# Order of VectorE and TensorE work in the first block of a two-block transformer kernel: convolution taps, pooling products, output product

## The chip, the cores and the metric

The kernel runs on one core of a Trainium2 chip. The metric is the device time of one execution in microseconds (us). The engines that matter here are TensorE (PE, matrix products, with a separate row PEld for loading weights), VectorE (DVE), ScalarE (ACT) and the queue of SyncE (SP), which issues the loads of weights. Each engine takes its instructions from a queue of its own; engines wait for each other by semaphores.

## The reference

The reference is a hybrid layer (the first block) followed by two more layers (the second block), on 512 tokens of width 1024, in float32. Only the mixing part of the first block is touched by the change:

```
h = rms_norm(x, norm1_g)
z = h @ w_in                       # split into 9 parts of 256 columns
y_pool  = pool_mixer(z_pool)       # moving means over 2, 4, 8, 16 tokens, then a 64x64 product per group
y_sconv = s_b * causal_dwconv(s_c * s_h, sconv_w)      # 3 taps
u       = causal_dwconv(c_a * sigmoid(c_g), conf_dw_w) + conf_dw_b    # 31 taps, each channel by itself
y_conf  = silu(layer_norm(u))
y_attn  = diff_attention(zq, zk, zv)                   # 4 heads, causal, two softmaxes per head
x = x + concat(y_pool, y_sconv, y_conf, y_attn) @ w_out
x = x + (silu(rms_norm(x) @ w_gate) * (rms_norm(x) @ w_up)) @ w_down
```

## The kernel before, in words

Activations are held with features on the 128 partitions and tokens along the free axis, so a stream of 256 features is two tiles `[:, 0]` and `[:, 1]` of 128x512. Every float32 product on TensorE is made of three passes: weight and activation are each split into a rounded part (`whi`, `hhi`) and a rest (`wlo`, `hlo`), and hi*hi, hi*lo and lo*hi are summed in PSUM. The split of weights is a ScalarE cast (L139) and a VectorE subtraction (L140, `wlo<-wraw,whi`); there are four buffers each of `whi` and `wlo`.

`layer1` works through the first block in this order: the gated stream of the 31-tap convolution (`u`), then the projections of values, keys and queries (L173, token-major), then the pooling stream `z`, the three streams of the short convolution, then the first output product `add_out(mixed[:4])`, which adds the pooling and short-convolution parts to `x`, and the second one, `add_out(mixed[4:])`, for attention (`yT`, mixed[4] and [5]) and convolution (`y`, mixed[6] and [7]). `mix` casts and splits such a part (L112 on ScalarE, L113 on VectorE) before it enters the output product. Each output product has 8 output tiles of 12 matmuls (4 parts x 3 passes), 96 matmuls in all, on three PSUM buffers `mm`; each tile ends in an addition to `x` on VectorE (L304).

Attention runs in the background: its stages are generators in `self.bg`, and `tick()`, called between groups of matmuls, lets the next stage emit its instructions. For keys and queries these are `heads_norm` (L484 to L486), `heads_stack` (`st`, L496 to L498) and `heads_turn` (transposes, L184 `psb<-keep,st`); after that, for each of 16 pairs of query block and head, `logits` (L536, then the VectorE pass L538 and the ScalarE exp L540), `turn` (transposes of `e`, copied to `pT`), `values` (`pso<-vtok,pT`, and for the last head of a block the normalisation of `ot`) and `finish` (transposes of `ot`, then `yT`, L590).

The 31-tap convolution `y` is one ScalarE instruction for the first tap and 30 VectorE instructions (L605) for the others, for each of the two tiles; 60 VectorE taps in all, each reading and writing the same `y`. When they are done comes a chain of its own, called the closing chain here: the sum over features on TensorE (L659, `psb<-y`), subtraction of the mean (L662), squares (L663), their sum (L667), the reciprocal root (L202 to L219), its spread over partitions (L223), and the scaling with SiLU (L674 to L678).

A scheduler decides at build time, from program order, priorities (`first()` and `chain()` raise them) and dependences, in which order each engine's queue stands; at run time each queue goes in that order. Tiles with a name in a pool are buffers in a ring: PSUM tiles `psb` have two buffers, handed out in program order, and the closing chain of `y`, the pooling product, and the transposes of attention all use them.

## Time and profile before

| what | us |
| --- | --- |
| median of 3 runs | 1217.9 (1216.07 to 1218.35) |
| time of the profiled execution | 1222.06 |
| its span, first to last instruction | 1220.3 |
| TensorE busy in the span | 1195.1 |
| VectorE busy in the span | 809.1 |
| ScalarE busy in the span | 622.0 |
| mean granted TensorE clock, share of full speed | 0.991 |

The profile gives for each engine its busy time, for each instruction its start and duration, and for an engine that sat idle what ended the wait. "Busy" on TensorE counts overlapping records, so TensorE is called busy where it is fed without a gap; what one matmul takes of TensorE's time is the distance from its start to the next one's.

### The profile page before, as it was taken

What the parts mean: (1) busy time and instruction counts of PE and PEld (TensorE: products, weight loads), DVE (VectorE), ACT (ScalarE), POOL (GpSimd) and SP (SyncE); (2) the same over time, 40 slices, a digit from 0 to 9 for tenths busy, and PEclk for the clock granted to TensorE, in tenths of its full rate; (3) what the DMA queues carried; (4) which work ended last, traced back from release to release, by engine and by line L of the source; (5) the groups of instructions that cost most, each with busy time, mean ns of one, the idle gap of its engine ahead of it and who ended that gap; (6) DMA issues with size and microseconds to landing.
All of it is one profiled execution on the core that took longest, in us unless ns stands there. A gap on an engine that the chain in (4) does not pass through costs nothing.

```text
span 1220.3 us, 18958 instructions
## 1 busy us (share of the span) xinstructions
PE 1195.1 (98%) x7234; PEld 1022.5 (84%) x7234; DVE 809.1 (66%) x1834; ACT 622.0 (51%) x1382; POOL 51.1 (4%) x77
## 2 busy tenths in 40 slices
PE   8989899999999999999999999999999999999996
PEld 6978788888888888888999899898899889876776
DVE  6899966444433444455799899666575576775775
ACT  6378656333323333344453345656563575575754
POOL 7000002000000000011000000000020000000000
PEclk9999999999999999999999999999999999999998
DMA  7422123223223332234221122222132213220122
GB/s 235 114 70 70 37 68 104 89 101 101 74 95 113 101 102 88 84 96 127 73 70 61 36 78 79 71 71 64 59 103 91 87 53 105 70 70 18 52 69 70
DMA packets 33308, 101.28 MB, mean 83 GB/s; under 512 B 4048, under 2 KB 6640, under 8 KB 33216
## 3 DMA queue, kind: packets, MB, share of 16 engines
q1 hardware_dynamic: 30528, 95.66, 24.6%
q0 software_dynamic: 880, 2.25, 0.7%
q10 hardware_dynamic: 1808, 2.16, 0.5%
q8 instruction: 57, 0.93, 0.3%
q14 instruction: 35, 0.29, 0.1%
HBM read 95.87 MB, written 3.10 MB: 81 GB/s over the span
## 4 chain that ended last, share of the span: by engine, by line
PE 86%; DVE 9%; ACT 3%; DMA 1%; issue 1%; SPq 0%; DVEq 0%; ACTq 0%
PE mm L154 68%; PE psb L184 3%; DVE wlo L140 2%; DVE y L605 2%; PE pso L1265 1%; DMA wraw<-in_w 1%; DVE sc L874 1%; PE pso L1018 1%; DVE m L873 1%; ACT whi L139 1%; PE psa L1146 1%; PE pso L1020 1%; PE pso L566 1%; PE mm L173 1%; DVE qk L749 1%
## 5 line engine op out<-in xcount | busy, mean ns | idle before, releaser
L154 PE MATMUL mm<-hhi,whi 128*128 128x512 f32 (+2 forms) x1280 | 432.8, 338 | 0.0
L154 PE MATMUL mm<-hlo,whi 128*128 128x512 f32 (+2 forms) x1280 | 427.5, 334 | 0.0
L154 PE MATMUL mm<-hhi,wlo 128*128 128x512 f32 (+2 forms) x1280 | 427.0, 334 | 0.0
L139 ACT CAST whi<-wraw 128x512 fp32r<-128x512 f32 x350 | 207.6, 595 | 328.4 <-PE mm L154 297.1
L140 DVE TENSOR_TENSOR wlo<-wraw,whi 128x512 fp32r<-128x512 f32 x350 | 233.9, 672 | 153.5 <-ACT whi L139 127.4
L154 PEld LDWEIGHTS mm<-hhi,whi 128*128 128x128 f32 x1280 | 242.4, 189 | 23.9 <-issue 2.2
L154 PEld LDWEIGHTS mm<-hlo,whi 128*128 128x128 f32 x1280 | 242.3, 189 | 21.8 <-issue 0.8
L154 PEld LDWEIGHTS mm<-hhi,wlo 128*128 128x128 f32 x1280 | 242.1, 189 | 21.8
L154 PE MATMUL mm<-mx,whi 128*128 128x512 f32 (+2 forms) x448 | 113.5, 342 | 3.5 <-ACT mx L112 3.3
L154 PEld LDWEIGHTS mm<-mx,whi 128*128 128x128 f32 x448 | 76.7, 192 | 15.7 <-ACT mx L112 4.1
L710 DVE TENSOR_TENSOR gu<-mm,rb 128x512 f32<-128x512 f32 x44 | 30.4, 691 | 68.8 <-PE mm L154 67.0
L154 PE MATMUL mm<-mx,wlo 128*128 128x512 f32 (+2 forms) x224 | 75.0, 335 | 0.0
L154 PE MATMUL mm<-hidh,wlo 128*128 128x512 f32 x176 | 68.5, 389 | 0.0
L154 PE MATMUL mm<-hidh,whi 128*128 128x512 f32 x176 | 68.5, 389 | 0.0
L154 PE MATMUL mm<-hidl,whi 128*128 128x512 f32 x176 | 68.5, 389 | 0.0
L247 POOL TENSOR_TENSOR acc<-acc,sq 128x528 f32<-128x528 f32 (+1 forms) x18 | 25.7, 1426 | 806.6 <-ACT sq L245 489.5
L316 DVE TENSOR_TENSOR tmp<-mm,rb 128x272 f32<-128x272 f32 (+2 forms) x76 | 35.6, 468 | 24.0 <-PE mm L154 22.8
L304 DVE TENSOR_TENSOR x<-x,mm 128x272 f32<-128x272 f32 (+2 forms) x72 | 36.7, 509 | 14.4 <-PE mm L154 13.2
L154 PEld LDWEIGHTS mm<-mx,wlo 128*128 128x128 f32 x224 | 42.8, 191 | 3.6
L605 DVE SCALAR_TENSOR_TENSOR y<-u,cols,y 128x512 f32<-128x512 f32 x60 | 42.5, 747 | 0.2
L154 PEld LDWEIGHTS mm<-hidh,wlo 128*128 128x128 f32 x176 | 33.0, 188 | 6.9
L154 PEld LDWEIGHTS mm<-hidh,whi 128*128 128x128 f32 x176 | 33.0, 188 | 6.9
(406 smaller groups left out, 1819.6 us busy)
## 6 DMA issues: line engine op xcount, KB each, us to landing
wraw<-in_w SPq DMA_DIRECT2D x145, 512.0 KB, 3.5
wraw<-in_w SPq DMA_DIRECT2D x16, 384.0 KB, 2.9
wraw<-in_w SPq DMA_DIRECT2D x16, 320.0 KB, 2.8
bh<-tab SPq DMA_DIRECT2D x16, 132.0 KB, 2.9
mx<-cqk SPq DMA_DIRECT2D x8, 132.0 KB, 2.4
x<-in_x SPq DMA_DIRECT2D x4, 256.0 KB, 7.3
x<-in_x ACTq DMA_DIRECT2D x4, 256.0 KB, 4.6
B<-tab POOLq DMA_DIRECT2D x4, 256.0 KB, 8.2
```

The lines of the kernel that those rows point to most:

```text
L139: self.nc.scalar.copy(hi[:, :w], raw[:, c])
L140: self.lo.tensor_tensor(out=lo[:, :w], in0=raw[:, c], in1=hi[:, :w].bitcast(F32), op=OP.subtract)
L154: nc.tensor.matmul(ps[b], lhsT=ww[i][:, f0:f0 + nf], rhs=aa[:, t0:t1], start=first and i == 0 and j == 0, stop=last and i == n - 1 and j == 2)
L173: nc.tensor.matmul(part(t), lhsT=aa[:, t0:t0 + nt], rhs=ww[i], start=u + i + j == 0 and t % 2 == 0, stop=u == 1 and i == 3 and j == 2, ski ...
L184: self.nc.tensor.transpose(out, in_, self.ident[:n, :n])
L247: e.tensor_tensor(out=acc[:, c0:c1], in0=acc[:, c0:c1], in1=sq[:, c0:c1], op=OP.add)
L304: nc.vector.tensor_tensor(out=x, in0=x, in1=p, op=OP.add)
L316: self.nc.vector.tensor_tensor(out=out[:, t0:t1], in0=p, in1=rb[:nf, t0:t1], op=OP.mult)
L566: nc.tensor.matmul(o[:, h * 64:h * 64 + 64], lhsT=pT[:, j * 128:(j + 1) * 128], rhs=vt[:, j, h * 64:h * 64 + 64], start=j == 0, stop=j == i)
L605: nc.vector.scalar_tensor_tensor(y[:, f], u[:, f, k:k + S], cw[:, f, k:k + 1], y[:, f], op0=OP.mult, op1=OP.add)
L710: nc.vector.tensor_tensor(out=t[:, g], in0=ps, in1=rbx, op=OP.mult)
L749: nc.vector.tensor_tensor(out=ll[a:a + 64], in0=src, in1=hh[r:r + 64].bitcast(F32), op=OP.subtract)
```

## The change

The arithmetic and the number of instructions of each kind stay as they are. What changes is the program order, and with it the order of the queues. (1) The taps of the convolution are emitted by `filler`, called from every `tick()`, at a pace given by a table (tick number, taps done); each is held, by a dependence that costs no semaphore, behind the VectorE instruction that stood last two ticks before. Taps that remain after the last projection are emitted together. (2) The sums and products of pooling are emitted before the short convolution's streams instead of after them. (3) `add_out` can begin with two output tiles at once, parts 0 and 1 of both first, then parts 2 and 3; both output products of the first block use it.

```
     def tick(self):
+        if self.filler:
+            self.filler()
         while self.bg:
...
+    def behind(self, ins, name):
+        if name and name != ins.ins.name:
+            self.tc.add_manual_dep(ins.ins, name, mybir.DependencyInfo(mybir.DependencyClass.NoSync, mybir.DependencyReason.DATA), reason="order")
...
+            if halves and u == 0:
+                (t0, t1), = toks
+                early = {f: [self.mm()[:, :t1 - t0]] for f in range(per)}
+                for h in range(2):
+                    for f in range(per):
+                        for i in range(h * nk // 2, (h + 1) * nk // 2):
+                            ah, al = mixed[i]
+                            for j, (ww, aa) in enumerate(((w[0], ah), (w[1], ah), (w[0], al))):
+                                nc.tensor.matmul(early[f][0], lhsT=ww[i][:, f * 128:f * 128 + 128], rhs=aa[:, t0:t1],
+                                                 start=i == 0 and j == 0, stop=i == nk - 1 and j == 2)
+                            self.tick()
...
+            taps = [(f, k) for f in range(2) for k in range(1, 31)]
+            paced = [(0, 0), (16, 14), (32, 28), (48, 35), (64, 40), (112, 60)]
+            done = []
+            def tap():
+                f, k = taps.pop(0)
+                return nc.vector.scalar_tensor_tensor(y[:, f], u[:, f, k:k + S], cw[:, f, k:k + 1], y[:, f], op0=OP.mult, op1=OP.add)
+            def filler():
+                done.append(self.last(mybir.EngineType.DVE))
+                t = len(done)
+                goal = np.interp(t, *zip(*paced))
+                while taps and 60 - len(taps) < goal:
+                    self.behind(tap(), done[-3] if t > 2 else None)
...
-            for f in range(2):
-                nc.scalar.activation(y[:, f], u[:, f, 0:S], AF.Identity, scale=cw[:, f, 0:1], bias=cb[:, f:f + 1])
-                for k in range(1, 31):
-                    nc.vector.scalar_tensor_tensor(y[:, f], u[:, f, k:k + S], cw[:, f, k:k + 1], y[:, f], op0=OP.mult, op1=OP.add)
...
             fproj(z[:, :, PADP:])
...
             fproj(None, evac=lambda f, ps: nc.scalar.copy(sc[:, f, PADS:], ps))
+            for f in range(2):
+                ps = self.ch("b")
+                nc.tensor.matmul(ps, lhsT=pw[:, f], rhs=z[:, f, PADP:], start=True, stop=True)
+                k = COLS["pscale"][0] + f
+                nc.scalar.mul(z[:, f, PADP:], ps, self.cols[:, k:k + 1])
+                mixed[f] = self.mix(z[:, f, PADP:], M, T)
             fproj(None, evac=lambda f, ps: nc.vector.tensor_tensor(out=sc[:, f, PADS:], in0=ps, in1=sc[:, f, PADS:], op=OP.mult))
             fproj(sb)
+            self.filler = None
+            while taps:
+                tap()
...
-            self.add_out(mixed[:4], X)
+            self.add_out(mixed[:4], X, halves=True)
...
-            self.add_out(mixed[4:], X, after)
+            self.add_out(mixed[4:], X, after, halves=True)
```

The queues of the changed kernel differ from those of before in the first block alone, and hold the same number of instructions of each kind there. Line numbers move: taps stand at L605 before and L509 now, weight splits at L140 and L152, matmuls at L154 and L166 (L319 where the two tiles are begun together), L484 to L497 become L535 to L548, L659 becomes L705, L667 becomes L713, L223 becomes L235, L184 becomes L196, L566 becomes L617, L304 becomes L332.

The first place is on VectorE, where the first stack of keys is prepared: `qss` is the sum of squares of a key half, `ktok` the normalised keys, `st` the stack that TensorE's transposes wait for. Before:

```order
L605 SCALAR_TENSOR_TENSOR y<-u,cols,y 128x512 [waits DVE_49] x5
L140 TENSOR_TENSOR wlo<-wraw,whi 128x512 [waits DMAHW5_49,PE_49,Activation_49]
L140 TENSOR_TENSOR wlo<-wraw,whi 128x512 [waits PE_49,Activation_49]
L605 SCALAR_TENSOR_TENSOR y<-u,cols,y 128x512 [waits DVE_49]
L605 SCALAR_TENSOR_TENSOR y<-u,cols,y 128x512
L605 SCALAR_TENSOR_TENSOR y<-u,cols,y 128x512 [waits DVE_49] x3
L484 TENSOR_REDUCE qss<-qsq 128x16 [waits Activation_49]
```

The same place on VectorE in the changed kernel, up to the same reduction:

```order
L509 SCALAR_TENSOR_TENSOR y<-u,cols,y 128x512 [waits DVE_49] x6
L152 TENSOR_TENSOR wlo<-wraw,whi 128x512 [waits DMAHW5_49,PE_49,Activation_49]
L152 TENSOR_TENSOR wlo<-wraw,whi 128x512 [waits PE_49,Activation_49]
L509 SCALAR_TENSOR_TENSOR y<-u,cols,y 128x512 [waits DVE_49] x4
L535 TENSOR_REDUCE qss<-qsq 128x16 [waits Activation_49]
```

Counted from the start, 28 taps stood ahead of this reduction and 25 do now; the number of weight splits ahead of it is the same.

The second place is on VectorE, between the last logits of attention (`e,st<-psa`, shown as ISA) and the first weights of the first output product. Before, from the last logits pass on (`sb` is the short convolution's last stream, and `mx<-sb,mx`, `mx<-z,mx` are second halves of `mix`):

```order
L538 ISA e,st<-psa,B_272 128x512 [waits PE_49]
L538 ISA st 128x1
L547 SCALAR_TENSOR_TENSOR e<-e,rd 128x512 [waits DVE_49]
L219 SCALAR_TENSOR_TENSOR os<-rt,ry 128x4 [waits DVE_49]
L646 TENSOR_TENSOR sb<-sb,mx 128x512
L578 TENSOR_TENSOR ot<-ot,os 128x256 [waits DVE_49]
L545 RECIPROCAL rd<-st 128x2 [waits Activation_49]
L645 SCALAR_TENSOR_TENSOR mx<-mx,cols 128x512
L113 TENSOR_TENSOR mx<-sb,mx 128x512 [waits Activation_49]
L546 TENSOR_SCALAR rd<-rd,st,rowp 128x1 [waits DVE_49]
L440 TENSOR_TENSOR sb<-mm,rb 128x512 [waits PE_49]
L547 SCALAR_TENSOR_TENSOR e<-e,rd 128x512 [waits DVE_49]
```

In the changed kernel, from the last logits pass to the first weight split:

```order
L589 ISA e,st<-psa,B_272 128x512 [waits PE_49]
L589 ISA st 128x1
L598 SCALAR_TENSOR_TENSOR e<-e,rd 128x512 [waits DVE_49]
L629 TENSOR_TENSOR ot<-ot,os 128x256 [waits DVE_49]
L698 TENSOR_TENSOR sb<-sb,mx 128x512
L596 RECIPROCAL rd<-st 128x2 [waits Activation_49]
L468 TENSOR_TENSOR sb<-mm,rb 128x512 [waits PE_49]
L125 TENSOR_TENSOR mx<-sb,mx 128x512 [waits Activation_49]
L597 TENSOR_SCALAR rd<-rd,st,rowp 128x1 [waits DVE_49]
L698 TENSOR_TENSOR sb<-sb,mx 128x512 [waits DVE_49]
L598 SCALAR_TENSOR_TENSOR e<-e,rd 128x512 [waits DVE_49]
L152 TENSOR_TENSOR wlo<-wraw,whi 128x512 [waits DMAHW7_49]
```

One step of the short convolution (L645) is out of this stretch; the weight split still stands behind both products of `sb` and the last `e`. After it four taps were left in the kernel before; in the changed one 13 are left, two at a time between the additions to `x` of the first output product.

The third place is on TensorE, in the first output product (`mm<-mx`), where the sum over features of `y` (`psb<-y`) and the sum of its squares (`psb<-ones,ysq`) stand. Before, this was after 21 of the 96 matmuls, and matmuls stood between the steps:

```order
L659 MATMUL psb<-y,m_107 128x512 [waits DVE_49]
L154 MATMUL mm<-mx,whi 128x512 x2
L154 MATMUL mm<-mx,wlo 128x512
L154 MATMUL mm<-mx,whi 128x512 x2
L154 MATMUL mm<-mx,wlo 128x512
L154 MATMUL mm<-mx,whi 128x512 x2
L667 MATMUL psb<-ones,ysq 128x1 [waits Activation_49]
L154 MATMUL mm<-mx,wlo 128x512
L154 MATMUL mm<-mx,whi 128x512
L667 MATMUL psb<-ones,ysq 128x1 [waits Activation_49]
```

In the changed kernel the same steps stand after 92 of the 96 matmuls:

```order
L705 MATMUL psb<-y,m_107 128x512 [waits DVE_49]
L166 MATMUL mm<-mx,wlo 128x512
L166 MATMUL mm<-mx,whi 128x512 x2
L166 MATMUL mm<-mx,wlo 128x512
L713 MATMUL psb<-ones,ysq 128x1 [waits PE_49,Activation_49]
L713 MATMUL psb<-ones,ysq 128x1 [waits Activation_49]
L713 MATMUL psb<-ones,ysq 128x1 x6
L235 MATMUL psb<-keep,yr 128x128 [waits DVE_49]
L235 MATMUL psb<-keep,yr 128x128 x3
```

Behind these rows TensorE's queue goes on with the last two transposes of `e`, the last two products with the values, the last transposes of `ot`, and only then the second output product, whose first matmul waits for the cast of `yT`:

```order
L196 MATMUL psb<-keep,e 128x128 [waits DVE_49]
L196 MATMUL psb<-keep,e 128x128 x3
L617 MATMUL pso<-vtok,pT 128x64 [waits Activation_49]
L617 MATMUL pso<-vtok,pT 128x64 x3
L617 MATMUL pso<-vtok,pT 128x64 [waits Activation_49]
L617 MATMUL pso<-vtok,pT 128x64 x3
L196 MATMUL psb<-keep,ot 128x128 [waits DVE_49,PE_49]
L196 MATMUL psb<-keep,ot 128x128
L319 MATMUL mm<-mx,whi 128x512 [waits Activation_49]
```

Before, 52 of the 96 matmuls of the first output product stood behind the last product with the values; now none does.

## Rows read from the trace of the kernel before

**Rows 1.** Page, busy time of TensorE and its weight loads in the span:

```profile
PE 1195.1 (98%) x7234; PEld 1022.5 (84%) x7234; DVE 809.1 (66%) x1834; ACT 622.0 (51%) x1382; POOL 51.1 (4%) x77
```

**Rows 2.** Waits of TensorE, whole span: us in total, times, longest:

```profile
PE mm L154 <- ACT mx L112: 3.3, 1, 3.3
PE psb L184 <- ACT st L498: 3.1, 1, 3.1
```

**Rows 3.** Busy by stretch: PE, PEld, DVE, ACT, POOL, granted clock, DMA share, GB/s:

```profile
64.00:68.00 4.00, 0.90 (x9) 0.84 (x9) 4.00 (x11) 3.19 (x10) 0.00 (x0) 1.00 0.32 124
68.00:72.00 4.00, 4.00 (x24) 4.00 (x23) 4.00 (x7) 1.95 (x5) 0.00 (x0) 0.57 0.43 131
148.00:152.00 4.00, 3.82 (x8) 2.62 (x9) 3.96 (x8) 0.63 (x2) 0.00 (x0) 0.50 0.39 131
152.00:156.00 4.00, 4.00 (x15) 3.17 (x15) 2.98 (x5) 0.62 (x1) 0.00 (x0) 0.80 0.42 131
155.81:175.28 19.47, 19.47 (x107) 15.80 (x106) 11.99 (x24) 12.51 (x28) 0.00 (x0) 1.00 0.16 52
205.00:1205.00 1000.00, 995.01 (x6126) 853.35 (x6127) 628.42 (x1428) 484.00 (x1060) 18.45 (x17) 1.00 0.25 79
```

**Rows 4.** VectorE in order of time before the first stack: start, us, instruction:

```profile
51.11 4.73 DVE L605 SCALAR_TENSOR_TENSOR y<-u,cols,y 128x512 f32<-128x512 f32 x7
56.95 3.40 DVE L605 SCALAR_TENSOR_TENSOR y<-u,cols,y 128x512 f32<-128x512 f32 x5
60.27 0.68 DVE L484 TENSOR_REDUCE qss<-qsq 128x16 f32<-128x512 f32 x1
66.25 0.42 DVE L497 TENSOR_TENSOR st<-ktok,st 128x256 fp32r<-128x256 f32 x1
```

**Rows 5.** TensorE at the first stack, in order of time:

```profile
67.17 1.09 PE L184 MATMUL psb<-keep,st 128*128 128x128 f32 x8 [3.10 <-ACT st L498]
```

**Rows 6.** VectorE after the last logits, in order of time:

```profile
140.54 0.68 DVE L538 CUSTOM_DVE_ANT_0 e<-psa,B 128x512 f32<-128x512 f32 x1
143.21 0.73 DVE L645 SCALAR_TENSOR_TENSOR mx<-mx,cols 128x512 f32<-128x512 f32 x1
146.86 1.29 DVE L140 TENSOR_TENSOR wlo<-wraw,whi 128x512 fp32r<-128x512 f32 x2
```

**Rows 7.** TensorE from the last logits to the first output product, in order of time:

```profile
139.15 0.71 PE L536 MATMUL psa<-kT,qT 128*128 128x512 f32 x2
141.09 1.88 PE L650 MATMUL psb<-z,pw 128*128 128x512 f32 x4
148.17 2.03 PE L154 MATMUL mm<-mx,whi 128*128 128x512 f32 x3 [3.32 <-ACT mx L112]
```

**Rows 8.** Chain that ended last, merged: start, TensorE's time, what:

```profile
155.97 0.86 PE psb L659 x2
159.49 1.46 PE psb L667 x14
162.45 0.61 PE psb L223 x4
163.98 0.52 PE psb L184 x4
165.42 0.87 PE pso L566 x8
208.33 131.72 PE mm L154 x581
```

**Rows 9.** The closing chain and attention's last block, in order of time:

```profile
155.81 1.02 PE L659 MATMUL psb<-y,m 128*128 128x512 f32 x2
167.67 0.42 DVE L574 TENSOR_TENSOR ot<-pso,rd 128x256 f32<-128x256 f32 x1 [3.29 <-PE pso L566]
169.63 0.63 ACT L195 ACTIVATE ysq<-ysq 128x512 f32<-128x512 f32 x1
174.81 0.47 ACT L590 ACTIVATE yT<-psb,cols 128x256 f32<-128x256 f32 x1 [0.29 <-PE psb L184]
```

More of the change, by code (lines that the diff above doesn't have):

```diff
@@ L100, in finish, with last @@
             self.tick()
+    def last(self, engine):
+        return next((i.name for i in reversed(self.nc.cur_bb.bb.instructions) if i.engine == engine), None)
+    def behind(self, ins, name):
+        if name and name != ins.ins.name:
+            self.tc.add_manual_dep(ins.ins, name, mybir.DependencyInfo(mybir.DependencyClass.NoSync, mybir.DependencyReason.DATA), reason="order")
     def row(self, name):
@@ L288, in mix, with add_out @@
         return hi, lo
-    def add_out(self, mixed, toks, after=None, ws=None):
+    def add_out(self, mixed, toks, after=None, ws=None, halves=False):
         nc = self.nc
@@ L296, in add_out @@
             w = ws[u] if ws else self.weights(nk, per * 128)
-            for f in range(per):
-                ps = [self.mm()[:, :t1 - t0] for t0, t1 in toks]
-                self.f_acc(ps, w, f * 128, 128, mixed, toks)
+            early = {}
+            if halves and u == 0:
[9 more added lines that the diff above has]
+                            self.tick()
+            for f in range(per):
+                if early:
+                    ps = early[f]
+                else:
+                    ps = [self.mm()[:, :t1 - t0] for t0, t1 in toks]
+                    self.f_acc(ps, w, f * 128, 128, mixed, toks)
                 kt = u * per + f
@@ L611, in layer1 @@
             fproj(z[:, :, PADP:])
-            rb2 = p.tile([128, S], F32, name="rb2")
-            nc.scalar.square(rb2, rbx)
-            PADS = 2
-            sb, sc, sh = G(S, "sb", "qtok"), X2(PADS + S), X2(S)
-            nc.gpsimd.memset(sc[:, :, :PADS], 0.0)
-            fproj(None, evac=lambda f, ps: nc.scalar.copy(sc[:, f, PADS:], ps))
-            fproj(None, evac=lambda f, ps: nc.vector.tensor_tensor(out=sc[:, f, PADS:], in0=ps, in1=sc[:, f, PADS:], op=OP.mult))
-            fproj(sb)
             mixed = [None] * 8
@@ L639, in layer1 @@
                     nc.vector.tensor_tensor(out=z[:, f, PADP:], in0=a[:, PADP:], in1=z[:, f, PADP:], op=OP.subtract)
+            rb2 = p.tile([128, S], F32, name="rb2")
+            nc.scalar.square(rb2, rbx)
+            PADS = 2
+            sb, sc, sh = G(S, "sb", "qtok"), X2(PADS + S), X2(S)
+            nc.gpsimd.memset(sc[:, :, :PADS], 0.0)
+            fproj(None, evac=lambda f, ps: nc.scalar.copy(sc[:, f, PADS:], ps))
+            for f in range(2):
+                ps = self.ch("b")
[3 more added lines that the diff above has]
+                mixed[f] = self.mix(z[:, f, PADP:], M, T)
+            fproj(None, evac=lambda f, ps: nc.vector.tensor_tensor(out=sc[:, f, PADS:], in0=ps, in1=sc[:, f, PADS:], op=OP.mult))
+            fproj(sb)
+            self.filler = None
+            while taps:
+                tap()
+            with self.chain():
                 nc.vector.tensor_tensor(out=sc[:, :, PADS:], in0=sc[:, :, PADS:], in1=rb2[:, None, :].to_broadcast([128, 2, S]), op=OP.mult)
@@ L647, in layer1 @@
                     mixed[2 + f] = self.mix(sb[:, f], M, T)
-            for f in range(2):
-                ps = self.ch("b")
-                nc.tensor.matmul(ps, lhsT=pw[:, f], rhs=z[:, f, PADP:], start=True, stop=True)
-                k = COLS["pscale"][0] + f
-                nc.scalar.mul(z[:, f, PADP:], ps, self.cols[:, k:k + 1])
-                mixed[f] = self.mix(z[:, f, PADP:], M, T)
             ones = self.m1
```

8 lines of the change are left out of this document (5 added, 3 removed).

## The prediction

> **What bounds the kernel now.** I read the page first: TensorE is busy 1195.1 of 1220.3 us [rows 1]. After the first block it is fed without a gap, 995.01 of 1000 us between 205 and 1205 [rows 3], so time lost or won in the first block is neither made up nor lost again later; the end moves by just that much. The waits of TensorE come next. Two are above 3 us, both in the first block: 3.1 for the first stack of keys and 3.3 for the first part of the output product [rows 2]. The windows then show what follows each: the granted clock is at 0.57 in 68 to 72 and at 0.50 and 0.80 in 148 to 156 [rows 3], that is TensorE at the lower of its two levels (1.2 instead of 2.4 GHz) for a while after it starts again. That costs 4 x 0.43 = 1.7 us after the first wait and 4 x 0.50 + 4 x 0.20 = 2.8 after the second. The two waits with their aftermath are 1.7 + 3.1 = 4.8 and 2.8 + 3.3 = 6.1 us, 10.9 in all, which is the most that a better order can win here. Third, I read where the closing chain of the convolution runs: from the sum over features at 155.81 [rows 9] to the last piece of attention, yT, at 174.81 + 0.47 = 175.28. In this stretch TensorE is busy 19.47 of 19.47 us [rows 3]: the chain is long, but matmuls of the first output product stand between its steps.
>
> **The change, part by part.** No instruction is added or dropped, so each term is a wait that shrinks or appears.
>
> *Taps paced, first wait.* VectorE works without a pause before the first stack: five taps from 56.95 to the reduction at 60.27 are 0.66 us each [rows 4]. In the new order 3 of 28 taps stand behind that reduction, so it starts 2.0 earlier. From it to the start of the transposes were 67.17 - 60.27 = 6.9 us [rows 4, 5]. In this stretch ScalarE's queue now has small operations of the second half of the keys ahead of the first copy of the stack; I take 0.5 of the 2.0 as lost to them, so that the transposes start 1.5 earlier. Three matmuls of the query projection moved from ahead of the transposes to behind them; half of 131.72 / 581 = 0.227 us [rows 8] each, 0.34 together, so the wait begins that much earlier. The wait shrinks by 1.5 - 0.34 = 1.1, to 2.0 us. Bounds: 0.6 (another 0.5 lost) and 1.7. Whether the lower clock still follows a wait of 2.0 us no row shows; the bounds are 0 and 1.7 won, and I take 0.8. Term: -1.1 - 0.8.
>
> *Pooling first, two tiles at once: second wait.* Before, the wait ended when the casts of the pooling parts came, which stood last; now parts 0 and 1 are there early. But the first matmul with wlo needs the split of the weights on VectorE, and in the new order that split still stands behind the whole tail of the last logits. Before, the last logits pass started at 140.54 and the split at 146.86, 6.3 later [rows 6]. One step of the short convolution, 0.73, and about 0.5 of small waits around it go out of the stretch: 5.1. Counted from TensorE's last logits at 139.15 [rows 7], the split starts at 1.4 + 5.1 = 6.5 and is done 0.65 later (half of 1.29), at 7.2. TensorE had 5.7 us of work of its own from there (to 148.17 - 3.32 = 144.85). Of this the pooling products (1.88 by their row [rows 7], of which I take 1.7, since the end overlaps with what follows) and half of the sum of y, 0.9 as the other half [rows 8], are now done earlier at the same price, and four matmuls with parts 0 and 1 come in, 0.9: 4.0 us. It waits 7.2 - 4.0 = 3.2 instead of 3.3 [rows 7]. The cover was brought forward together with the work that it would cover. Term: -0.2, with a little for a short second wait; bounds 0 and -6.1, if the wait closes with its aftermath.
>
> *Taps held back: the closing chain.* 13 taps are left for the first output product instead of 4, and VectorE's queue puts them between the additions to x, so the sum over features stands behind 92 of the 96 matmuls. TensorE's queue then holds the steps of the chain one after another, then the last transposes and products of attention, which share the two buffers psb with them, then the second output product. I add up the path from the start of the sum over features:
> - to the end of the spread of the reciprocal root: 162.45 + 0.61 - 155.81 = 7.25 [rows 8, 9], and 0.15 since a cast of weights that waits for the end of the product now stands ahead of the squares on ScalarE: 7.4;
> - to the end of the last product with the values: 167.67 - 163.06 = 4.6 before; 4.4 without casts of weights in between;
> - to yT: 175.28 - 167.67 = 7.6 before [rows 9]. One addition to x and three weight splits on VectorE (about 0.6 each) stand elsewhere now: 5.2;
> - the cast of yT, as long as another 128x512 pass on ScalarE: 0.63 [rows 9].
>
> That is 17.6 us. TensorE's own work in it: 0.86 for the sum, four matmuls 0.9, 16 sums of squares at 1.46 / 14 = 1.7, the spread 0.61, 12 transposes at 0.52 / 4 = 1.6, 16 products at 0.87 / 8 = 1.7 [rows 8], together 7.4. It stands idle for 17.6 - 7.4 = 10.2 us. Bounds: 7.5 if four passes of y's SiLU between attention's steps (some 0.65 each) delay nothing, and 12.7 if the path is as long as before (175.28 - 155.81 + 0.63 = 20.1). A row for the clock after broken work like this is missing; the nearest are the 1.7 and 2.8 us after the two waits, and I take 2.2, with 0 and 2.8 as bounds. Term: +10.2 + 2.2.
>
> That VectorE comes to the last tap in time I check by a sum: 13 taps at 0.66, seven additions and eight splits at about 0.6 make 17.6 us against 92 matmuls at 0.227 = 20.9, so TensorE's pace sets the start of the chain and no more is lost there.
>
> Behind a matmul that waits, nothing runs on TensorE: in the 3.10 us ahead of the transposes [rows 5] the query projection's matmuls stood ready behind them. The Trainium skill (PSUM - Partial Sum Buffer, Engine vs sequencer instructions) states the same as a rule, matmuls start and complete in program order. It speaks against this change: by it the products of attention that stand behind the closing chain cannot fill its waits. If they could pass, the sum would be lower by about the 4.4 us of the second step; I keep the sum by the rows.
>
> **Sum.** -1.1 - 0.8 - 0.2 + 10.2 + 2.2 = +10.3 us. The profiled execution took 1222.06 us for a span of 1220.3, 4.2 above the median; the terms are differences, so I put the sum on the median: 1217.9 + 10.3 = 1228.2. With all bounds one way (the closing of the second wait is a rival, below) the forecast's own range is -1.7 - 1.7 - 0.2 + 7.5 = +3.9 to -0.6 + 12.7 + 2.8 = +14.9, 1222 to 1233.
>
> **The rivals.**
> - *The second wait closes.* If the split of the first weights comes before TensorE needs it (it decides below 4.0 us after the last logits' start, where I have 7.2), 6.1 are won instead of 0.2: 1222.3. For it: pooling's parts are ready early. Against: the order of VectorE's queue. Chance 0.12.
> - *The closing chain stays hidden, and the change wins.* If TensorE finds the steps ready as it did before, with no wait in 19.47 us [rows 3], the 12.4 us fall away, the first wait's -1.9 to -2.8 stays: 1215 to 1216, faster. It decides where the path from the sum to yT's cast is below 9.5 us. Against: 17.6 by the rows, and only four matmuls stand between. Chance 0.05.
> - *The waits only change places.* Path at its low bound and no lower clock (+7.5), second wait closed (-6.1), first wait as forecast (-1.9): 1217.4, no change. Chance 0.05.
> - *VectorE is late.* If the 13 taps end after TensorE's 92 matmuls (17.6 us become more than 21), the chain starts later, by some 3 us: 1231. For it: VectorE is busy through all of 64 to 72 [rows 3] and has little slack in this block. Against: the sum above. Chance 0.08.
>
> **How the numbers follow.** The forecast has 0.70. A difference under 0.2%, 2.4 us, can't be told from no change. Faster by more than that: half of the second rival and the low end of the first, 0.04. Within: the rest of the second and the third: 0.08. Slower: all else, 0.88. The range, 1221.5 to 1232.5, takes in the first rival's centre and most of the fourth, and leaves out the other two.
>
> **What would show it.** Right: among TensorE's waits one or more around the end of the first output product, together about 10 us, for ScalarE and VectorE steps of y and ot; the longest before the last transposes of ot and before the first matmul of the second product; a lower granted clock right behind it; the first wait at about 2 us; the wait at the start of the first output product still about 3 us, now for wlo on VectorE. The prediction fails if TensorE passes the closing chain with under 6 us of waits, or if the wait for the first weights is gone.

## The result, and the profile after

The changed kernel took 1235.05 us (median of 4 runs, 1231.56 to 1240.64) against 1218.12 for the kernel before (4 runs): a ratio of 1.0139, interval 1.0114 to 1.0164. It is slower by 17 us. The two profiled executions lie closer together: span 1232.1 against 1220.3 us, 11.8 more.

The waits of TensorE in the changed kernel, first those that answer to [rows 2] and then those around the end of the first output product (us in total, times, longest):

```profile
PE psb L196 <- DVE ot L629: 4.3, 1, 4.3
...
PE psb L196 <- ACT st L549: 2.2, 1, 2.2
PE mm L319 <- DVE wlo L152: 2.0, 1, 2.0
...
PE psb L235 <- DVE yr L231: 1.5, 1, 1.5
...
PE mm L319 <- ACT mx L124: 1.2, 1, 1.2
...
PE psb L713 <- ACT ysq L709: 1.0, 1, 1.0
PE mm L166 <- DVE sb L468: 0.9, 1, 0.9
PE psb L196 <- ACT yT L641: 0.6, 1, 0.6
PE psb L196 <- ACT e L591: 0.4, 1, 0.4
```

The first wait (`st`) shrank from 3.1 to 2.2. The second one, 3.3 for a cast of `mx` before, is now 0.9 for `sb` and 2.0 for the split `wlo`. The other six are new. The one of 0.4 for `e` ends at 101.05, in an earlier part of attention; the five around the end of the first output product are 4.3 + 1.5 + 1.2 + 1.0 + 0.6 = 8.5 us (added unrounded). TensorE in order of time shows where they stand, from the end of the first output product to the start of the second:

```profile
172.02 1.02 PE L705 MATMUL psb<-y,m 128*128 128x512 f32 x2
...
174.97 2.24 PE L713 MATMUL psb<-ones,ysq 128*128 128x1 f32 x16 [1.00 <-ACT ysq L709]
178.68 1.07 PE L235 MATMUL psb<-keep,yr 128*128 128x128 f32 x4 [1.46 <-DVE yr L231]
...
180.73 1.77 PE L196 MATMUL psb<-keep,e 128*128 128x128 f32 x8 [0.56 <-ACT yT L641]
182.52 2.11 PE L617 MATMUL pso<-vtok,pT 128*128 128x64 f32 x16
188.94 0.66 PE L196 MATMUL psb<-keep,ot 128*128 128x128 f32 x2 [4.31 <-DVE ot L629]
190.82 0.79 PE L319 MATMUL mm<-mx,whi 128*128 128x512 f32 x1 [1.21 <-ACT mx L124]
```

The second piece of the sum over features stood at 155.81 with matmuls of the product around each step of the chain [rows 9]; now it stands at 172.02, and the product ends before the chain does. The windows (columns as in [rows 3]; the third number from the right is the granted clock) show what that does to the clock:

```profile
64.00:68.00 4.00, 1.91 (x9) 1.91 (x10) 3.98 (x10) 3.08 (x10) 0.00 (x0) 0.76 0.05 22
68.00:72.00 4.00, 4.00 (x31) 4.00 (x30) 3.27 (x6) 2.21 (x6) 0.00 (x0) 0.81 0.43 131
148.00:152.00 4.00, 2.61 (x6) 2.13 (x7) 4.00 (x8) 0.62 (x1) 0.00 (x0) 0.50 0.14 19
152.00:156.00 4.00, 4.00 (x13) 3.11 (x13) 1.27 (x3) 0.62 (x1) 0.00 (x0) 0.64 0.72 243
176.00:180.00 4.00, 2.54 (x17) 2.22 (x17) 0.55 (x3) 0.88 (x4) 0.00 (x0) 0.84 0.41 131
180.00:184.00 4.00, 3.42 (x21) 2.97 (x21) 1.06 (x2) 3.29 (x7) 0.00 (x0) 0.73 0.00 0
184.00:188.00 4.00, 0.63 (x6) 0.49 (x5) 2.16 (x5) 3.85 (x11) 0.00 (x0) 0.70 0.00 0
188.00:192.00 4.00, 1.84 (x5) 1.25 (x6) 1.93 (x6) 2.33 (x5) 0.00 (x0) 0.50 0.00 0
192.00:196.00 4.00, 4.00 (x12) 3.08 (x11) 1.29 (x3) 0.33 (x1) 0.00 (x0) 0.52 0.02 4
```

From 176 to 196 the granted clock is between 0.84 and 0.50, that is at its lower level for most of that time, with a return to full speed around 184. Such windows also give an account of the whole span. In steps of 4 us I add up TensorE's idle time (length less busy) and the time lost to the lower clock (busy x (1 - clock); in 192 to 196, 4.00 x 0.48 = 1.9). What is left of the span should be the same work at full clock in every trace of the same kernel. In the two kernels that were traced twice, and in two others, it agrees to 0.4 us:

| trace | span | idle 56-224 | lower clock 56-224 | lower clock elsewhere | idle elsewhere | left |
| --- | --- | --- | --- | --- | --- | --- |
| before | 1220.3 | 6.6 | 4.6 | 2.1 | 18.6 | 1188.4 |
| before, second trace | 1220.3 | 8.2 | 4.5 | 0.1 | 19.0 | 1188.5 |
| changed | 1232.1 | 14.6 | 8.3 | 1.7 | 19.2 | 1188.3 |
| changed, second trace | 1231.2 | 12.5 | 7.1 | 3.6 | 19.4 | 1188.6 |
| taps done by tick 64 | 1223.3 | 10.0 | 3.9 | 1.7 | 19.5 | 1188.2 |
| attention first, late pace | 1222.5 | 4.5 | 3.2 | 7.2 | 19.1 | 1188.5 |

In the other seven kernels without added matmuls what is left lies between 1186.8 and 1190.6, so from kernel to kernel this account closes within some 2 us, not within tenths.

The 11.8 us between the first two traces are 8.0 of idle time in the first block, 3.7 of lower clock there, and small change elsewhere (0.6 idle, -0.4 lower clock).

### The profile page after: what moved, and what is told of

Same layout as the page of the kernel before. It is cut to its first block, busy times and chain, and to the rows that moved or that the text cites. A ratio compares the mean times of both kernels' runs of the same rounds, so it can differ in the third digit from the quotient of the medians.

```text
span 1232.1 us, 18962 instructions
## 1 busy us (share of the span) xinstructions
PE 1198.2 (97%) x7234; PEld 1024.7 (83%) x7234; DVE 812.9 (66%) x1834; ACT 622.7 (51%) x1382; POOL 51.2 (4%) x77
## 4 chain that ended last, share of the span: by engine, by line
PE 85%; DVE 9%; ACT 4%; DMA 1%; issue 1%; SPq 0%; DVEq 0%; ACTq 0%
PE mm L166 66%; PE psb L196 4%; DVE wlo L152 2%; DVE y L509 1%; PE pso L1311 1%; PE mm L319 1%; DMA wraw<-in_w 1%; DVE sc L920 1%; PE pso L1064 1%; DVE m L919 1%; PE psa L166 1%; ACT whi L151 1%; PE psa L1192 1%; PE pso L1066 1%; DVE qk L795 1%
## 5 line engine op out<-in xcount | busy, mean ns | idle before, releaser
L166 PE MATMUL mm<-hhi,whi 128*128 128x512 f32 (+2 forms) x1280 | 432.6, 338 | 0.0
L166 PE MATMUL mm<-hlo,whi 128*128 128x512 f32 (+2 forms) x1280 | 426.9, 334 | 0.0
L166 PE MATMUL mm<-hhi,wlo 128*128 128x512 f32 (+2 forms) x1280 | 426.2, 333 | 0.0
L152 DVE TENSOR_TENSOR wlo<-wraw,whi 128x512 fp32r<-128x512 f32 x350 | 234.1, 673 | 155.1 <-ACT whi L151 128.9
L166 PEld LDWEIGHTS mm<-hhi,whi 128*128 128x128 f32 x1280 | 241.7, 189 | 24.1 <-issue 2.4
L166 PEld LDWEIGHTS mm<-hlo,whi 128*128 128x128 f32 x1280 | 241.6, 189 | 22.2 <-issue 1.1
L166 PEld LDWEIGHTS mm<-hhi,wlo 128*128 128x128 f32 x1280 | 241.4, 189 | 21.8
L166 PE MATMUL mm<-mx,whi 128*128 128x512 f32 (+2 forms) x416 | 100.0, 331 | 1.1 <-DVE sb L468 0.9
L166 PEld LDWEIGHTS mm<-mx,whi 128*128 128x128 f32 x416 | 69.6, 189 | 10.4 <-issue 3.1
L166 PE MATMUL mm<-hidh,whi 128*128 128x512 f32 x176 | 68.5, 389 | 0.0
L166 PE MATMUL mm<-hidl,whi 128*128 128x512 f32 x176 | 68.5, 389 | 0.0
L166 PE MATMUL mm<-hidh,wlo 128*128 128x512 f32 x176 | 68.5, 389 | 0.0
L166 PE MATMUL mm<-mx,wlo 128*128 128x512 f32 (+2 forms) x208 | 68.0, 328 | 0.0
L332 DVE TENSOR_TENSOR x<-x,mm 128x272 f32<-128x272 f32 (+2 forms) x72 | 36.7, 510 | 14.5 <-PE mm L166 9.8
L509 DVE SCALAR_TENSOR_TENSOR y<-u,cols,y 128x512 f32<-128x512 f32 x60 | 44.9, 748 | 1.0
L166 PEld LDWEIGHTS mm<-mx,wlo 128*128 128x128 f32 x208 | 39.3, 189 | 3.2 <-issue 0.2
L166 PEld LDWEIGHTS mm<-hidh,whi 128*128 128x128 f32 x176 | 33.0, 188 | 6.9
L166 PEld LDWEIGHTS mm<-hidl,whi 128*128 128x128 f32 x176 | 33.0, 188 | 6.8
```

The source lines that it names most:

```text
L152: self.lo.tensor_tensor(out=lo[:, :w], in0=raw[:, c], in1=hi[:, :w].bitcast(F32), op=OP.subtract)
L166: nc.tensor.matmul(ps[b], lhsT=ww[i][:, f0:f0 + nf], rhs=aa[:, t0:t1], start=first and i == 0 and j == 0, stop=last and i == n - 1 and j == 2)
L332: nc.vector.tensor_tensor(out=x, in0=x, in1=p, op=OP.add)
L509: return nc.vector.scalar_tensor_tensor(y[:, f], u[:, f, k:k + S], cw[:, f, k:k + 1], y[:, f], op0=OP.mult, op1=OP.add)
```

## The experiments

The theory: the taps that are held back put the closing chain of `y` behind nearly all matmuls that covered it, so its waits, and those of attention's last steps behind it in TensorE's queue, are exposed. The rivals: pooling's new place costs it, the two tiles at once cost it, or the lower clock does by itself. Medians of the kernel before beside each group of runs are given with it.

**1. Undo one part, or delay it less** (before: 1218.99). The first kernel takes `filler` out and puts the taps back to where they stood; the second takes the two tiles away; the third changes the pace; the fourth the place of attention's last steps.

```
+            for f in range(2):
+                nc.scalar.activation(y[:, f], ...)
+                for k in range(1, 31):
+                    nc.vector.scalar_tensor_tensor(y[:, f], u[:, f, k:k + S], ...)
```

> The changed kernel with the taps emitted as before; pooling first and the two tiles at once stay. TensorE's queue has the sum over features after 43 of the 96 matmuls of the first output product instead of after 92. If the late closing chain costs the time: 53 matmuls x 0.227 = 12.0 us and TensorE's own 7.4 us in the chain cover 19.4 us, against a path of 18.6 us measured in the changed kernel, so at most some 2 us of waits are left there: 1216 to 1222 us. If pooling's new place or the two tiles at once cost it (or the lower clock that follows their waits): 1230 us and more.

Measured 1220.69, ratio 1.0014 (1.0002 to 1.0026): 14 of the 17 us are gone with the pacing alone undone. One wait above 1 us is left at the end of the first output product (1.2 for the cast of `yT`), and at its start 0.8 for `sb`.

```
-            self.add_out(mixed[:4], X, halves=True)
+            self.add_out(mixed[:4], X)
-            self.add_out(mixed[4:], X, after, halves=True)
+            self.add_out(mixed[4:], X, after)
```

> The changed kernel without the two tiles at once in both output products. The sum over features still stands after 92 of 96 matmuls. If the late closing chain costs the time: 1232 to 1237 us, about 10 us of waits around the end of the first output product as in the changed kernel. If the two tiles at once cost it: 1226 us or less.

Measured 1234.32, ratio 1.0120 (1.0104 to 1.0137), with waits of 3.8, 1.5, 1.2 and 1.0 in the chain: the two tiles at once neither cost nor win anything to be measured.

```
-            paced = [(0, 0), (16, 14), (32, 28), (48, 35), (64, 40), (112, 60)]
+            paced = [(0, 0), (16, 14), (32, 28), (48, 44), (64, 60)]
```

> The changed kernel with a faster pace table, 60 taps at tick 64 instead of 40: TensorE's queue has the sum over features after 71 of 96 matmuls instead of after 92. If the waits of the closing chain cost the time, 21 matmuls more cover 21 x 0.227 = 4.8 us: 1229 to 1231 us, with about 5 us of waits left around the end of the first output product. If it is the lower clock after any such waits, or something elsewhere in the block, and not the length of the waits: 1234 to 1237 us.

Measured 1225.40, ratio 1.0058 (1.0043 to 1.0074): 4 us better than the theory had it. Its waits of TensorE:

```profile
PE psb L196 <- DVE ot L629: 4.5, 1, 4.5
...
PE psb L196 <- ACT st L549: 2.8, 1, 2.8
...
PE mm L319 <- ACT mx L124: 1.2, 1, 1.2
...
PE mm L166 <- DVE sb L468: 0.6, 1, 0.6
```

In the chain 5.7 us are left, as forecast. By the windows the chain with its lower clock takes 4.8 us less than in the changed kernel, 3.0 of idle time and 1.8 of clock. What I had not seen is the start of the first output product: the wait for `wlo` is gone. VectorE's rows there, first of the changed kernel, then of this one (in both the wait was for the first `wlo`):

```profile
147.99 0.74 DVE L598 SCALAR_TENSOR_TENSOR e<-e,rd 128x512 f32<-128x512 f32 x1
148.65 0.68 DVE L152 TENSOR_TENSOR wlo<-wraw,whi 128x512 fp32r<-128x512 f32 x1
```

```profile
147.01 0.67 DVE L152 TENSOR_TENSOR wlo<-wraw,whi 128x512 fp32r<-128x512 f32 x1
...
148.99 0.74 DVE L598 SCALAR_TENSOR_TENSOR e<-e,rd 128x512 f32<-128x512 f32 x1
```

TensorE's last logits and its first matmul with `wlo`, again first of the changed kernel, then of this one:

```profile
142.23 0.71 PE L587 MATMUL psa<-kT,qT 128*128 128x512 f32 x2
...
149.39 0.79 PE L319 MATMUL mm<-mx,wlo 128*128 128x512 f32 x1 [2.03 <-DVE wlo L152]
```

```profile
143.00 0.71 PE L587 MATMUL psa<-kT,qT 128*128 128x512 f32 x2
...
147.74 0.51 PE L319 MATMUL mm<-mx,wlo 128*128 128x512 f32 x1
```

With the taps out of the way sooner the split stands ahead of the last step of the logits: it starts 4.0 us after TensorE's last logits instead of 6.4, and is done after 4.7 instead of 7.1. That is the rival "the second wait closes". Its condition (done below 4.0 us) was a little too strict: at 4.7 TensorE no longer waits for the split, in part because it waits 0.6 for `sb` before it. By the windows from 140 to 156 the closed wait and the clock behind it, 1.00 here, are worth 5.1 us.

```
+            self.finish(att)
             ones = self.m1
             with self.chain():
...
             self.add_out(mixed[:4], X, halves=True)
-            self.finish(att)
```

> The changed kernel with the last steps of attention emitted ahead of y's closing chain; the taps stay as late as in the changed kernel, and the sum over features stands after 87 of 96 matmuls. If attention's steps standing behind y's waiting ones in TensorE's queue cost the time: the waits before the last transposes of ot and the second product go, matmuls of the second product stand between y's steps, and what is left is a wait of 3 to 4 us for the cast of y (only 6 matmuls, 1.4 us, between the spread of the reciprocal root and the first use of y, against a path of about 5) and 1 to 2 us for ot: 1221 to 1228 us. If the late end of the taps alone sets it, whatever stands behind: 1233 to 1237 us.

Measured 1224.84, ratio 1.0048 (1.0030 to 1.0065). The taps end as late as in the changed kernel, yet 10 us come back, and the wait of 3 to 4 us forecast for the cast of `y` is there with 4.7:

```profile
PE mm L319 <- ACT mx L124: 4.7, 1, 4.7
```

By the windows about 7 of these us come back from 172 on: there the loss is not the late chain alone but also what stood behind its waiting steps in TensorE's queue. About 4 come back at the start of the first output product, which I had not foreseen. The last products with the values now stand ahead of the first `wlo`, which TensorE no longer waits for, and the clock stays up:

```profile
149.17 1.10 PE L617 MATMUL pso<-vtok,pT 128*128 128x64 f32 x8 [0.67 <-ACT pT L607]
150.09 0.48 PE L319 MATMUL mm<-mx,wlo 128*128 128x512 f32 x1
```

```profile
148.00:152.00 4.00, 3.33 (x20) 2.76 (x20) 3.85 (x8) 1.82 (x4) 0.00 (x0) 1.00 0.33 93
```

**2. Second traces, filled waits, and both remedies** (before: 1218.70).

> The kernel before, unchanged, for a second trace of it. The first one was 4.2 us above the median and had three stretches at the lower clock (after the two waits, and at 638 to 642). If those stretches come and go from run to run: an execution near 1218 us has the same two waits of 3.1 and 3.3 us, but fewer or shorter stretches at the lower clock. If they belong to the kernel: the same three stretches, and the time differs for another reason.

One execution, 1222.12 us: waits of 4.1 and 3.3 (and 0.5 behind it), the lower clock behind both again, but none at 638 to 642.

> The changed kernel, unchanged, for a second trace and more runs of it beside the kernels below. Waits around the end of the first output product again 9 us in all. If the 5 us by which its median exceeds the forecast of the waits is the lower clock: stretches at the lower clock after the second wait and from 176 to 196 in every trace of it, 4 to 5 us of lost time together in the last, and the longer executions show the lower mean clock. Median 1233 to 1236.

Measured 1235.13, ratio 1.0132 (1.0109 to 1.0155). In the trace the chain's waits are 8.1 us, the wait for `st` is down to 0.5, and the clock is 0.50 from 176 to 192 with TensorE busy for 10.4 of 16 us. The longer executions have the lower mean clock (1238.04 and 1239.08 at 0.983, the others at 0.986 to 0.987).

```
+                    for _ in range(8):
+                        nc.tensor.matmul(d, lhsT=self.m1, rhs=pT, start=True, stop=True)
```

These stand behind the last product with the values; 3 more stand behind the sums of squares, 4 behind the last transposes of `ot`.

> The changed kernel with 15 matmuls added whose results nothing reads: 3 in the wait for yr, 8 in the wait for the last ot, 4 in the wait for the cast of yT, some 6 us of TensorE's time at full clock in about 7 us of its waits. No other engine's queue changes. If the granted clock falls because TensorE pauses there: it stays at 1.00 from 176 to 196, and of the 4.4 us that the lower clock takes there most come back, 1229 to 1232 us against 1235. If the clock falls for another reason, or the path alone sets the time: 1234 to 1237 us.

Measured 1235.51: no gain, but this run does not tell what the lower clock costs. The clock is 1.00 from 184 on in its trace, but the added matmuls took twice what I had reckoned with and were longer than the waits (three of them 4.4 us in a wait of 1.5).

The last kernel of this group has attention's last steps first, as above, and this pace:

```
-            paced = [(0, 0), (16, 14), (32, 28), (48, 35), (64, 40), (112, 60)]
+            paced = [(0, 0), (16, 14), (32, 28), (48, 44), (64, 60)]
```

> Attention's last steps ahead of y's closing chain (as in the run with attention first) and 60 taps done by tick 64 (as in the run with the faster pace): the sum over features after 59 matmuls of the first output product, the spread of the reciprocal root after 80, so about 20 matmuls, 5 us, more cover the path to the cast of y. If the closing chain and what stands behind it in TensorE's queue are the whole cost of the change: the 4.7 us wait for the cast of y and its lower clock go, 1216 to 1219 us, no slower than before. If pooling's new place or the two tiles at once cost something of their own: 1221 us and more, with waits at another place.

Measured 1221.89, ratio 1.0020 (1.0006 to 1.0035), between the two expectations: 13 of 17 us come back, and waits of 2.5 (`st`) and 2.3 (cast of `y`) are left.

**3. One part alone, and the filled waits again** (before: 1219.60). The first two kernels put into the kernel before the pacing alone, then pooling's move alone; the third is the one with added matmuls, with 1, 4 and 2 of them; the fourth the first kernel of group 1 with attention first.

```
+            self.filler = filler
...
             fproj(sb)
+            self.filler = None
+            while taps:
+                tap()
```

> The kernel before with the paced taps alone; pooling stays behind the short convolution and no two tiles are begun at once. TensorE's queue has the sum over features after 51 of the 96 matmuls (21 before, 92 in the changed kernel). If the place of the sum in TensorE's queue sets the cost: 45 x 0.227 + 7.4 = 17.6 us of cover against a path of 18.6 to the last transposes and 1.2 more to the cast of yT, so 1 to 3 us of waits at the end of the first output product: 1218 to 1222 us. If holding the taps back costs by itself, wherever the sum stands: 1230 us and more.

Measured 1229.37, ratio 1.0086 (1.0065 to 1.0107): the expectation failed. The end of the first output product does what it said (2.1 and 1.2 us of waits), but its start does not:

```profile
PE mm L166 <- ACT mx L124: 4.8, 2, 3.6
...
PE mm L166 <- DVE wlo L152: 1.6, 1, 1.6
```

Paced taps alone make the second wait longer, 1.6 + 3.6 against 3.3 [rows 2]. Where it arises stands in VectorE's rows:

```profile
148.52 0.75 DVE L493 SCALAR_TENSOR_TENSOR y<-u,cols,y 128x512 f32<-128x512 f32 x1
149.18 0.69 DVE L452 TENSOR_TENSOR sb<-mm,rb 128x512 f32<-128x512 f32 x1
149.78 0.75 DVE L493 SCALAR_TENSOR_TENSOR y<-u,cols,y 128x512 f32<-128x512 f32 x1
150.44 0.69 DVE L675 TENSOR_TENSOR sb<-sb,mx 128x512 f32<-128x512 f32 x1
```

Leftover taps stand around the last steps of the short convolution, whose cast, and pooling's behind it, the product waits for. So the pacing alone makes 10 of the 17 us. The rest comes only with pooling's move, which shifts the sum over features from after 51 to after 92 matmuls.

```
             fproj(None, evac=lambda f, ps: nc.scalar.copy(sc[:, f, PADS:], ps))
+            for f in range(2):
+                ps = self.ch("b")
+                nc.tensor.matmul(ps, lhsT=pw[:, f], rhs=z[:, f, PADP:], start=True, stop=True)
...
```

> The kernel before with pooling's sums and products ahead of the short convolution and nothing else changed. The sum over features stands after 45 of 96 matmuls, so the closing chain is covered but for about 1 us. If the wait at the start of the first output product closes, as it did in the run without the paced taps: 1216 to 1220 us. If pooling's earlier place costs something of its own: 1222 us and more.

Measured 1219.97, ratio 1.0005 (0.9992 to 1.0019): pooling's place by itself costs nothing, and wins nothing either, though only 0.6 us are left of the second wait. Part of it comes back at the start of the second output product, as a wait of 1.2 for the cast of `yT`, and the mean clock of its 12 executions is 0.993, as that of the kernel before beside it.

```
-                    for _ in range(8):
+                    for _ in range(4):
                         nc.tensor.matmul(d, lhsT=self.m1, rhs=pT, start=True, stop=True)
```

> As the run with 15 added matmuls, but with 7, since each 128x512 one took 0.87 us of TensorE there and not the 0.43 that I had reckoned with: 1 in the wait for yr, 4 in the wait for the last ot, 2 in the wait for the cast of yT; 0.9, 3.5 and 0.9 us against waits of 1.5, 4.3 and 1.2, so none of them lengthens the path. If the lower clock costs time there because TensorE pauses: the granted clock is 1.00 from 184 on, and 2 to 4 us come back, 1231 to 1233 us. If the lower clock lies mostly beside the waits and costs little: 1234 to 1236 us.

Measured 1232.38, ratio 1.0117 (1.0094 to 1.0140), 2.7 below the changed kernel's 1235.1, and in its trace the clock stays up where it had been at 0.70 and 0.50:

```profile
184.00:188.00 4.00, 4.00 (x16) 2.12 (x15) 1.89 (x4) 3.94 (x11) 0.00 (x0) 1.00 0.00 0
188.00:192.00 4.00, 2.82 (x12) 1.83 (x12) 2.18 (x6) 2.48 (x6) 0.00 (x0) 1.00 0.00 0
```

From 176 to 184 it is still lower, at 0.88 and 0.69. The 2.7 us fit the price of the lower clock at this place, but they are not shown: the interval of this ratio and that of the changed kernel above (1.0109 to 1.0155) overlap for the most part.

```
+            self.finish(att)
             ones = self.m1
...
-            self.finish(att)
```

> Taps as before, pooling first, two tiles at once, and attention's last steps ahead of y's closing chain: in TensorE's queue the last transposes of ot stand after 28 and the sum over features after 32 matmuls of the first output product, with matmuls between all their steps. If waits that stand behind one another in TensorE's queue are all that the late chain costs: no wait above 1 us is left in either output product, 1215 to 1218 us, as fast as before or slightly faster. If a wait goes from here to another place: 1219 to 1223 us.

Measured 1220.07, ratio 1.0003 (0.9990 to 1.0017). A wait of 1.1 came up elsewhere (for `rd`, ended at 142.48), with the lower clock behind it (0.50 and 0.67 from 144 to 152): the second expectation.

**4. What was still open** (before: 1219.57). Three matmuls in the second wait of the kernel before, two in that of the kernel with 7 added matmuls, and, with attention's last steps first, a pace for the first wait:

```
+            d = self.ch("a")
+            for _ in range(3):
+                nc.tensor.matmul(d, lhsT=self.m1, rhs=z[:, 1, PADP:], start=True, stop=True)
             ones = self.m1
```

> The kernel before with three added matmuls, whose results nothing reads, in the wait of 3.3 us at the start of the first output product (0.87 us each, 2.6 in all). The sum over features moves from 21 to 29 of the 96 matmuls, which leaves the closing chain covered. If the lower clock behind that wait costs the kernel before 2.7 to 3.0 us in most executions, as in both its traces: 1215 to 1217 us, the granted clock 1.00 from 148 to 156. If it comes in few executions, or costs little: 1218 to 1220 us.

Measured 1217.39, ratio 0.9987 (0.9971 to 1.0002), 2.2 us less: near the first expectation, though the interval just takes in no change. Its trace has no lower clock in the block, and its 12 executions have a mean clock of 0.995 against 0.991 for the kernel before beside it.

```
+                if (i, h) == (3, 3):
+                    d = self.ch("a")
+                    for _ in range(2):
+                        nc.tensor.matmul(d, lhsT=self.m1, rhs=es[1], start=True, stop=True)
```

> The run with 7 added matmuls (1232.4 us), and two more in the wait of 2.0 us for the first split of weights at the start of the first output product. If the lower clock behind that wait costs 1.6 to 2.7 us, as in the traces of the changed kernel: 1230 to 1231 us. With it nearly all of the lower clock in the first output product's waits is gone, and what is left over the kernel before with its wait filled too is the length of the waits, 9 us of the closing chain less some 1 of the first wait, and a pause of 0.5 at attention: 8 to 9 us by the traces. If more than 12 us are left between the two, the lower clock is not what the waits leave unexplained.

Measured 1232.65: no gain. The lower clock behind the second wait is gone (1.00 in 148 to 156), but the two matmuls could start only with `e`, at 148.56, and 1.4 us of the wait came after them. And here the lower clock stayed in the chain, although the added matmuls kept TensorE busy:

```profile
184.00:188.00 4.00, 4.00 (x14) 2.97 (x14) 1.35 (x3) 3.04 (x8) 0.00 (x0) 0.50 0.00 0
```

The two runs differ by 15 us, more than the 12 that I had set as the limit; since the second still held 7.6 us of lower clock in the block, this pair does not separate the two.

```
+            paced = [(0, 0), (32, 16), (64, 60)]
```

> Attention's last steps ahead of y's closing chain, and a pace table that starts slowly and ends early (16 taps at tick 32, 60 at tick 64): 21 taps stand ahead of the first reduction of keys (25 in the changed kernel, 28 before), and the sum over features after 72 matmuls. If taps ahead of that reduction set the first wait: 4 x 0.66 = 2.6 us earlier, a first wait under 0.5 us with no lower clock behind it, and a wait of about 2 us for the cast of y as with the faster pace: 1217 to 1220 us. If VectorE's other work sets the first wait: 2 to 3 us there again, 1220 to 1224 us.

Measured 1219.00, ratio 0.9997 (0.9982 to 1.0011): the whole loss is gone. TensorE no longer waits for `st`; VectorE's first reduction and the stack come 4 us before those of [rows 4]:

```profile
56.08 0.69 DVE L535 TENSOR_REDUCE qss<-qsq 128x16 f32<-128x512 f32 x1 [0.43 <-ACT qsq L533]
...
62.16 0.42 DVE L548 TENSOR_TENSOR st<-ktok,st 128x256 fp32r<-128x256 f32 x1
```

No version was faster than the kernel before by more than could be told from no change.

## Why the prediction was right in its direction and wrong in its size

- *Closing chain, +10.2 of waits*: right in its mechanism, and 2 us too high. 8.5 and 8.1 us in the two traces: 4.3 before the last transposes of `ot` and 1.2 before the first matmul of the second product, as named, and 1.0, 1.5 and 0.6 at `ysq`, `yr` and `yT`. The path from the sum (172.18, where the chain that ended last has its first piece) to 190.82 is 18.6 us against 17.6. The rule of the Trainium skill (PSUM - Partial Sum Buffer, Engine vs sequencer instructions), that matmuls start in program order, agrees with it: with attention's steps ahead of the chain about 7 us come back at this place, the taps as late as before.
- *First wait, -1.1*: 0.9 won in the first trace, but that is within what the wait varies by. In six traces with 28 taps ahead of the reduction it is 2.2 to 4.1 (mean 2.9), in ten with 25 taps 0.3 to 4.1 (mean 2.6), and the reduction starts 0.4 us earlier on average, not 2.0. Only the last run, with 21 taps, lies outside: there the reduction starts earlier than in all others, and there is no wait.
- *Second wait, -0.2*: 2.9 against 3.3, so -0.4; the split was behind the logits' tail, as said, done 7.1 us after the last logits' start where 7.2 was forecast. The reason given, that the cover was brought forward, was only half of it: with the taps done sooner the wait nearly closes (0.6), and with the taps alone it grows (5.2). Held-back taps cost at both ends of the first output product, which no term had.
- *VectorE comes in time*: right for the last tap (the sum is not waited for), and too narrow, since the taps also squeeze the short convolution's last steps, in the run with the pacing alone.
- *Lower clock, -0.8 and +2.2*: the step that failed, by its size. The forecast added 1.4 us for it in all. In the chain it took 0.4 + 0.9 + 0.2 + 0.9 + 1.9 = 4.3 us in the windows from 176 to 196, and 5.5 in the second trace (172 to 192), beyond the bound of 2.8; behind the first wait it went on in the first trace (1.2 us, where 0.9 was forecast as left of 1.7). I had priced it from a single wait with full work behind it, and here the work behind the waits was itself broken into short pieces by further waits. Over the whole span it took 6.7 and 4.6 us in the two traces before and 10.0 and 10.7 in the two of the changed kernel. In the changed kernel's executions without a trace it cost still more, as the mean clocks tell: 0.984 on average over nine executions of the changed kernel (0.987 and 0.986 in its two traces), 0.992 over 81 of the kernel before (0.991 and 0.993). In the 17 traces of this study the account's lower clock grows by about 1.0 us for each 0.001 that the mean clock falls (0.2 us at 0.997, 15.3 at 0.984). By this estimate the changed kernel loses about 8 us more to the lower clock than the kernel before, where 1.4 was forecast. That is half of the 16 us between the mean times of these executions (1235.7 and 1219.5). The waits, forecast at -1.1 - 0.2 + 10.2 = +8.9, make up about the other half: the idle time in the block is 8.0 us more by the first pair of traces, and 4.3 by the second, where the first wait was long in the one before (4.1) and short in the changed one (0.5).
- *The sum put on the median*: the traces differ by 11.8 and 10.9 us, near the +10.3, but that nearness is in part luck. Both traces of the kernel before come from long executions (1222.06 and 1222.12, against medians of 1218 to 1220 and a low of 1215.38), those of the changed one from short ones (1233.86 and 1233.02, against 1235). For the changed kernel the mean clocks give the reason: its traced executions had less of the lower clock than most of its others. For the kernel before they do not: its traced executions have an ordinary mean clock and are still 2.7 us longer than the average. What makes them longer stays open.

## What to carry to other kernels

Before moving filler work later on one engine, follow what its end releases: here sixty small instructions were followed by a chain that needs half a product's matmuls as cover, and by another chain behind it in the same queue. Where such work must be late, put independent steps ahead of the waiting chain in the in-order queue, and pace the filler by what each consumer needs (in the last run few taps before the first stack, and the last tap at 163.7 us instead of 171.0 in the changed kernel). When terms come from one trace, find out where that execution stands among the others, in its time and in its mean clock, before the sum is put on a median.

## What the runs showed of the hardware that was not expected

Whether the lower clock follows a wait was not settled by the wait's length. Behind waits of 2.4 us for `st` it did not come in two traces (the kernel without pacing, and the one before with its second wait filled: 1.00 in 68 to 72), nor behind 3.3 us in the kernel with pooling's move alone (1.00 from 64 to 76), and behind 2.2 us in the changed kernel it did. It also came, in some traces and not in others, while TensorE was busy throughout, in the second block; of the run with the late pace:

```profile
668.00:672.00 4.00, 4.00 (x41) 3.19 (x39) 3.99 (x11) 1.45 (x7) 0.00 (x0) 0.86 0.38 121
672.00:676.00 4.00, 4.00 (x17) 3.33 (x17) 2.10 (x8) 0.50 (x2) 0.00 (x0) 0.50 0.04 16
...
684.00:688.00 4.00, 4.00 (x26) 3.09 (x25) 3.09 (x9) 0.73 (x3) 0.00 (x0) 0.93 0.48 135
```

Before it TensorE had waited 1.03 us, up to 664.90, and then run products with 16 rows or columns among others. These 20 us cost 6.8 us in this trace, and 684 to 700 as much in that of the kernel with 7 added matmuls. In both traces of before and both of the changed kernel the clock is 1.00 behind the same wait. That is more than several edits of this study are worth.
